# Two-partition block inversion, and transposes moved from TensorE to VectorE and DMA

## The chip, the cores and the metric

The kernel runs on one core of a Trainium2 chip. The metric is the device time of one execution in microseconds (us), taken as the median of several runs. A profile of one execution gives, for each engine, when each instruction ran and what it waited for. The engines are TensorE (PE in the profile; its weight loads are PEld), VectorE (DVE), ScalarE (ACT), GpSimd (POOL) and SyncE (SP, which here only issues transfers).

## The reference, cut to what matters

One step of a bidirectional hybrid layer: 384 tokens (128 context, 256 latent), width 2048, all in float32. An input projection feeds an RWKV-7 branch and a gated short convolution; both are projected, merged, projected again and added to the input. The scan is what the change touches, for 32 heads of size 64, in each of two directions:

```python
def step(S, inp):
    r_t, w_t, k_t, v_t, a_t, b_t = inp
    sa = jnp.einsum('dbhij,dbhj->dbhi', S, a_t)
    S = S * w_t[..., None, :] + sa[..., :, None] * b_t[..., None, :] + v_t[..., :, None] * k_t[..., None, :]
    y = jnp.einsum('dbhij,dbhj->dbhi', S, r_t)
    return S, y
```

The kernel computes it by chunks of 64 tokens. Inside a chunk the dependence of a token on the earlier ones is a strictly upper triangular 64x64 matrix, and the chunk needs the inverse of (identity minus that matrix).

## The kernel before, in words

**Two streams in one hand-written PE order.** A `Stream` object multiplies the activations with the weights (every product in three passes of float32r, `mm3`). One step of it is three matmuls of 128x128 by 384 columns; half a pair of weight columns is sixteen steps and one or two loads `raw` (1 MB together, `wload`, L96 to L106, two buffers), which ScalarE and VectorE split into a high and a low part (`whi`, `wlo`, L88 and L89, three buffers). The order of PE's instructions is the order of the program text; the other engines' order is made by a planner. The second stream is the scan, in sixteen blocks of two heads (128 channels). Its parts are generators: a `yield n` in them lets the weight stream do n steps (`drive`, L943). So the weight stream's steps stand between the scan's parts and hide their latencies.

**One block.** The main loop (L961) takes, in order:

- `prep_b` (L667): VectorE makes `pr` and `bk` (receptances and keys scaled by the decays), for two directions and six chunks each. PE multiplies them (`pA`, L703), VectorE masks the products into `A` (L709). The diagonal 32x32 blocks of A, 48 of them (two directions, two halves of a chunk, six chunks by two heads), are stored to a DRAM tile `ui` by SP (L713) and loaded back as `U` with one matrix on each of 48 partitions (L719). VectorE inverts there by thirty steps of two instructions, a product `ut` (L724) and an addition (L726). SP stores the inverses to `uo` (L729) and loads them into A (L734). VectorE then turns two of the four groups into `x11` (L737). GpSimd meanwhile multiplies `bk` by the chunk's last decay (L716).
- `prep_c` (L739): PE turns the values `v` (L763; reversed by a ScalarE copy, L760, for the second direction) and ten of the twelve key chunks of `bk` that the scan needs turned (L772); ScalarE copies both from PSUM into `sav` (L765) and `bt` (L773).
- `prep_a` of the next block (L608), after the stream has finished the pair `gv`; then the stream runs on until 80 steps (`WINDOW`) have gone by since `prep_b`.
- `scan` (L784): it begins with `pav` (L850), which reads the turned values, and `pH` (L842), the first matmul that reads `x11`; then come the chains over the chunks, which read `bt` (`pu`, L828). GpSimd clears part of A (L863).

`tc.issue_after(x)` makes what follows stand behind instruction x in the order of its engine.

Of the kernel before, what the change touches and what calls it, by code (L numbers as in the profile page):

```python
# [56 lines left out]
def hybrid_step(ctx, tc, cst, x_prompt, x_sample, state_f, state_b, c, c_ctx, ada_w, ada_b, norm_g,  # L57
# [38 lines left out]
    def wload(view, k0, cols, nm):  # L96

        w = P * len(cols)
        raw = wp.tile([P, 8, w], F32, tag="raw", name=f"raw_{nm}", bufs=2)
        if cols[-1] == cols[0] + P:  # L100
            nc.sync.dma_start(raw[:], view[:, k0:k0 + 8, cols[0]:cols[0] + 256])
        else:
            for i, c0 in enumerate(cols):
                nc.sync.dma_start(raw[:, :, i * P:(i + 1) * P], view[:, k0:k0 + 8, c0:c0 + P])
# [491 lines left out]
    def flat(a):  # L596
        return a.rearrange("p n t -> p (n t)")
# [4 lines left out]
    def hl_parts(t, hi, nm):  # L602
# [2 lines left out]
        V.tensor_tensor(lo[:], t[:], hi[:].bitcast(F32), ALU.subtract)  # L605
        return hi, lo

    def prep_a(b, o):  # L608

        bs = slice(b * P, (b + 1) * P)  # L610
        k = k_[b]
        kk = sp.tile([P, T], F32, tag="kk", name=f"kk_{b}")
        S.mul(kk[:], k[:], pcol(KK + b))
        sq = tmp(f"sq_{b}")
        S.activation(sq[:], kk[:], AF.Square)
        sqh, sql = hl_parts(sq, sp.tile([P, T], F32R, tag="hl", name=f"sqh_{b}"), f"sq_{b}")
# [50 lines left out]
    def prep_b(b, o):  # L667

        r, kk = r_[b], o["kk"]
        o["pr"], o["bk"] = [], []  # L670
        for d in range(2):
            ep, em, kd, bn = o["ep"][d], o["em"][d], o["kd"][d], o["bn"][d]
            pr = sp.tile([P, NCH, P], F32, tag=f"pr{d}", name=f"pr_{b}_{d}")
            bk = sp.tile([P, NCH, P], F32, tag=f"bk{d}", name=f"bk_{b}_{d}")
# [9 lines left out]
            o["bk"].append(bk)  # L684
        yield PB0

        def blocks(A, d, e):
# [9 lines left out]
        for d in range(2):  # L697
# [7 lines left out]
            for n0, w in ((0, 4), (4, 2)):  # L705
                mk = cs[:, m0:m0 + P].rearrange("p (w t) -> p w t", t=C).unsqueeze(1).broadcast_to([P, w, 2, C])
                for h in range(2):
                    f0 = NCH * d + n0
                    V.tensor_tensor(A[:, :, f0:f0 + w, hss[h]].rearrange("p w n t -> p n w t"),  # L709
                                    pas[h, n0][:, 0:w, :].rearrange("p n (w t) -> p n w t", t=C), mk, ALU.mult)  # L710
            yield PB1
            for e in range(2):
                nc.sync.dma_start(ui[d, e].rearrange("i s t -> s i t"), blocks(A, d, e))  # L713

        for d in range(2):
            G.tensor_tensor(o["bk"][d][:], o["bk"][d][:], o["ep"][d][:, :, C:C + 1].broadcast_to([P, NCH, P]), ALU.mult)  # L716

        U = sp.tile([48, 32, 32], F32, tag="U", name=f"U_{b}")
        nc.sync.dma_start(U[:], ui[:].rearrange("d e i s t -> (d e i) s t"))  # L719
        ut = sp.tile([48, 256], F32, tag="ut", name=f"ut_{b}")  # L720
        for s in range(1, 31):
            w = 31 - s
            tv = ut[:, 0:s * w].rearrange("p (a b) -> p a b", b=w)
            V.tensor_tensor(tv, U[:, 0:s, s:s + 1].broadcast_to([48, s, w]),  # L724
                            U[:, s:s + 1, s + 1:].broadcast_to([48, s, w]), ALU.mult)
            V.tensor_tensor(U[:, 0:s, s + 1:], U[:, 0:s, s + 1:], tv, ALU.add)  # L726
        dg = U[:].rearrange("p a b -> p (a b)")[:, 0:1024:33]
        V.tensor_scalar(dg, dg, 1.0, None, ALU.add)
        nc.sync.dma_start(uo[:].rearrange("d e i s t -> (d e i) s t"), U[:])  # L729
        x11 = sp.tile([64, 24, 32], F32, tag="x11", name=f"x11_{b}")  # L730
        o["x11"] = x11
        for e in range(2):
            for d in range(2):
                nc.sync.dma_start(blocks(A, d, e), uo[d, e].rearrange("i s t -> s i t"))  # L734

        for d in range(2):
            box["turned"] = V.transpose(x11[0:32, 12 * d:12 * d + 12, :], blocks(A, d, 0)).ins  # L737

    def prep_c(b, o):  # L739

        r, v, A = r_[b], v_[b], o["A"]

        s_in = sp.tile([P, 2, C], F32, tag="s_in", name=f"s_in_{b}")
        for d in range(2):
# [10 lines left out]
        for d in range(2):  # L755
            if d == 0:
                src = v
            else:
                src = tmp(f"vr_{b}")
                S.copy(src[:], v[:, ::-1])  # L760
            pv = bank(f"pv_{b}_{d}")
            for q in range(3):
                TE.transpose(pv[:, q, :], src[:, q * P:(q + 1) * P], ident)  # L763
# [3 lines left out]
        for d in range(2):  # L767

            for n0, n1 in (((0, 4), (4, 5)), ((0, 3), (4, 6)))[d]:
                pb = bank(f"pb_{b}_{d}_{n0}")  # L770
                for n in range(n0, n1):
                    TE.transpose(pb[:, n - n0, :], o["bk"][d][:, n, :], ident)  # L772
                S.copy(bt[:, NCH * d + n0:NCH * d + n1, :], pb[:, 0:n1 - n0, :])  # L773
                yield 1
# [397 lines left out]
```

## Time and profile before

| | us |
|---|---|
| median of 3 runs | 2236.57 (2234.74 to 2237.20) |
| the profiled execution | 2234.36 |
| its span, first to last instruction | 2232.6 |
| TensorE busy | 2173.1 (97%) |
| VectorE busy | 1553.3 (70%) |
| ScalarE busy | 1013.5 (45%) |
| GpSimd busy | 115.7 (5%) |

The mean granted TensorE clock is 0.998 of full speed. A row of a timeline has the start (us from the span's start), the duration in us, engine, line, operation, the tiles written and read, and in brackets the idle time before it with what ended that. A row of a group has the count after "x", then the busy time in us, the mean in ns, and the idle time before the group's instructions with its causes. Matmuls are pipelined, so that their listed durations overlap and only differences of starts tell what one costs.

### The profile page before, as it was taken

To read this page: it belongs to the slowest core of one execution; us is meant where nothing else is said; L and a number is where in the kernel's file an instruction comes from. 1 tells how busy PE (TensorE), PEld (TensorE's weight loads), DVE (VectorE), ACT (ScalarE), POOL (GpSimd) and SP (SyncE) were. 2 spreads that over 40 slices of the span, in tenths; PEclk is the share of its full clock that TensorE was granted. 3 is DMA by queue.
4 is the path that set the end of the run, shared out by engine and by line. 5 is a ranking of instruction groups with operands and counts; after the bars stand their busy time and mean duration, and the time that the engine had idled before them with its cause. 6 is when DMAs were issued, how large, how long until landed. Compare 5 with 4: busy or idle time off the path is not lost.

```text
span 2232.6 us, 40518 instructions
## 1 busy us (share of the span) xinstructions
PE 2173.1 (97%) x16020; PEld 2062.7 (92%) x16020; DVE 1553.3 (70%) x3240; ACT 1013.5 (45%) x1784; POOL 115.7 (5%) x113
## 2 busy tenths in 40 slices
PE   5999999999999999999999999999999999999998
PEld 3589999999999999999999999999999999998988
DVE  3259567787878878777878787887777785444354
ACT  4245435454545454444445454546454633333333
POOL 2000000000000000000000000000000000000000
PEclk9999999999999999999999999999999999999999
DMA  9974454444343435343444434344445464886633
GB/s 338 346 211 128 131 141 116 116 117 118 108 132 107 130 100 131 106 130 100 121 108 127 112 107 133 107 122 126 124 118 139 144 196 143 294 281 233 220 132 113
DMA packets 426574, 335.25 MB, mean 150 GB/s; under 512 B 82496, under 2 KB 408720, under 8 KB 425488
## 3 DMA queue, kind: packets, MB, share of 16 engines
q1 hardware_dynamic: 424896, 330.91, 50.2%
q8 instruction: 126, 2.06, 0.4%
q10 hardware_dynamic: 432, 1.57, 0.2%
q14 instruction: 64, 0.52, 0.1%
q0 software_dynamic: 1056, 0.19, 0.1%
HBM read 305.80 MB, written 26.21 MB: 149 GB/s over the span
## 4 chain that ended last, share of the span: by engine, by line
PE 74%; DVE 12%; DMA 6%; ACT 4%; issue 2%; SPq 1%; POOL 0%; POOLq 0%; DVEq 0%; ACTq 0%
DMA raw_adah<-in_ada_w_dram 4%; PE d_rk L81 3%; PE d_rk L82 3%; PE d_rk L83 3%; PE d_gv L81 3%; PE d_gv L82 3%; PE d_gv L83 3%; PE d_oa L81 2%; PE pA L703 2%; PE d_oa L83 2%; PE d_oa L82 2%; PE d_mb L81 2%; PE d_mb L83 2%; PE d_mb L82 2%; PE d_bc L81 2%
## 5 line engine op out<-in xcount | busy, mean ns | idle before, releaser
L724 DVE TENSOR_TENSOR ut<-U 48x30 f32<-48x30 f32 (+14 forms) x480 | 154.8, 323 | 18.3 <-DMA U<-ui 5.5
L81 PE MATMUL d_rk<-h_hi,whi_rk 128*128 128x384 f32 x480 | 161.7, 337 | 0.6 <-ACT lst L554 0.6
L726 DVE TENSOR_TENSOR U<-U,ut 48x30 f32<-48x30 f32 (+14 forms) x480 | 154.5, 322 | 11.1
L81 PE MATMUL d_gv<-h_hi,whi_gv 128*128 128x384 f32 x480 | 160.6, 335 | 0.0
L82 PE MATMUL d_rk<-h_lo,whi_rk 128*128 128x384 f32 x480 | 160.5, 334 | 0.0
L83 PE MATMUL d_rk<-h_hi,wlo_rk 128*128 128x384 f32 x480 | 160.4, 334 | 0.0
L83 PE MATMUL d_gv<-h_hi,wlo_gv 128*128 128x384 f32 x480 | 160.4, 334 | 0.0
L82 PE MATMUL d_gv<-h_lo,whi_gv 128*128 128x384 f32 x480 | 160.4, 334 | 0.0
L88 ACT CAST whi_gv<-raw_gv 128x1024 fp32r<-128x1024 f32 (+1 forms) x64 | 64.0, 999 | 139.6 <-PE d_rk L82 100.0
L88 ACT CAST whi_rk<-raw_rk 128x1024 fp32r<-128x1024 f32 x60 | 63.0, 1054 | 110.8 <-PE d_rk L82 34.7
L89 DVE TENSOR_TENSOR wlo_rk<-raw_rk,whi_rk 128x1024 fp32r<-128x1024 f32 x60 | 72.9, 1218 | 45.3 <-ACT whi_rk L88 35.6
L81 PE MATMUL d_bc<-h_hi,whi_bc 128*128 128x384 f32 x256 | 92.2, 360 | 0.0
L81 PE MATMUL d_gb<-h_hi,whi_gb 128*128 128x384 f32 x256 | 92.2, 360 | 0.0
L81 PE MATMUL d_bg<-h_hi,whi_bg 128*128 128x384 f32 x256 | 92.2, 360 | 0.0
L81 PE MATMUL d_bx<-h_hi,whi_bx 128*128 128x384 f32 x256 | 92.1, 360 | 0.0
L81 PE MATMUL d_ma<-h_hi,whi_ma 128*128 128x384 f32 x256 | 91.6, 358 | 0.0
L81 PEld LDWEIGHTS d_rk<-h_hi,whi_rk 128*128 128x128 f32 x480 | 90.1, 188 | 0.9 <-ACT lst L554 0.9
L81 PE MATMUL d_mb<-h_hi,whi_mb 128*128 128x384 f32 x256 | 90.4, 353 | 0.0
L81 PEld LDWEIGHTS d_gv<-h_hi,whi_gv 128*128 128x128 f32 x480 | 90.1, 188 | 0.2
L81 PE MATMUL d_ob<-ybh,whi_ob 128*128 128x384 f32 x256 | 88.4, 345 | 2.0 <-DVE smb L521 1.0
L82 PEld LDWEIGHTS d_rk<-h_lo,whi_rk 128*128 128x128 f32 x480 | 90.2, 188 | 0.0
L82 PEld LDWEIGHTS d_gv<-h_lo,whi_gv 128*128 128x128 f32 x480 | 90.1, 188 | 0.0
(315 smaller groups left out, 6548.4 us busy)
## 6 DMA issues: line engine op xcount, KB each, us to landing
raw_adah<-in_ada_w_dram SPq DMA_DIRECT2D x64, 512.0 KB, 8.7
raw_rk<-in_w_in_dram SPq DMA_DIRECT2D x60, 512.0 KB, 5.3
raw_gv<-in_w_in_dram SPq DMA_DIRECT2D x60, 512.0 KB, 4.9
raw_ma<-in_w_in_dram SPq DMA_DIRECT2D x16, 1024.0 KB, 5.6
raw_mb<-in_w_in_dram SPq DMA_DIRECT2D x16, 1024.0 KB, 5.6
raw_bc<-in_w_in_dram SPq DMA_DIRECT2D x16, 1024.0 KB, 5.5
raw_bx<-in_w_in_dram SPq DMA_DIRECT2D x16, 1024.0 KB, 5.4
raw_bg<-in_w_in_dram SPq DMA_DIRECT2D x16, 1024.0 KB, 5.5
```

What stands on the lines that cost most here:

```text
L81: TE.matmul(out, wh, xh, start=start, stop=False)
L82: TE.matmul(out, wh, xl, start=False, stop=False)
L83: TE.matmul(out, wl, xh, start=False, stop=stop)
L88: S.copy(hi[0:rows], src)
L89: V.tensor_tensor(lo[0:rows], src, hi[0:rows].bitcast(F32), ALU.subtract)
L703: TE.matmul(pas[h, n // 4 * 4][:, n % 4, :], bk[hss[h], n, :], pr[hss[h], n, :], start=True, stop=True)
L724: V.tensor_tensor(tv, U[:, 0:s, s:s + 1].broadcast_to([48, s, w]), U[:, s:s + 1, s + 1:].broadcast_to([48, s, w]), ALU.mult)
L726: V.tensor_tensor(U[:, 0:s, s + 1:], U[:, 0:s, s + 1:], tv, ALU.add)
```

## The change

- The 48 matrices are inverted on 96 partitions. `un` holds all rows of every matrix twice, on partitions 0 to 47 and 64 to 111; `ux` holds the even rows on the first group and the odd rows on the second. A step updates up to half as many rows in each partition. Four loads take the place of one, and the added diagonal takes two instructions.
- The inverses are stored by two transfers and loaded back by four, all issued by GpSimd instead of SP. `x11` lies in `un`.
- PE's sixteen transposes a block and the ScalarE copies behind them go. VectorE's 32x32 transposes turn the blocks of the values (into `vt`) and of all twelve key chunks (in place, in `bks`); SP then places the blocks with transfers from SBUF to SBUF: eight for the values (behind the loads of `ux`) and sixteen for the keys (four at a time, behind the latest weight load), each of 32 partitions by twelve runs of 128 bytes.
- `prep_c` lets the weight stream go on 24 and 16 steps before the first and the second half of the key transfers, where it had seven single steps in all.

```diff
@@ wload @@
+                x = nc.sync.dma_start(raw[:, :, i * P:(i + 1) * P], view[:, k0:k0 + 8, c0:c0 + P])
+        box["raw"] = x.ins
@@ before prep_a @@
+    un = sp.tile([112, 32, 32], F32, tag="un", name="un")
+    ux = sp.tile([112, 16, 32], F32, tag="ux", name="ux")
+    G.memset(un[:], 0.0)
+    G.memset(ux[:], 0.0)
@@ prep_b @@
+        bks = sp.tile([P, 2, NCH, P], F32, tag="bk", name=f"bk_{b}")
+        o["bk"] = [bks[:, d] for d in range(2)]
...
+        vt = sp.tile([P, 2, T], F32, tag="vt", name=f"vt_{b}")
+        with tc.issue_after(last):
+            for d in range(2):
+                V.transpose(vt[:, d], v_[b][:, ::-1] if d else v_[b][:])
+            for d in range(2):
+                V.transpose(flat(bks[:, d]), flat(bks[:, d]))
-        U = sp.tile([48, 32, 32], F32, tag="U", name=f"U_{b}")
-        nc.sync.dma_start(U[:], ui[:].rearrange("d e i s t -> (d e i) s t"))
+        for g in range(2):
+            nc.sync.dma_start(un[64 * g:64 * g + 48], ui[:].rearrange("d e i s t -> (d e i) s t"))
+        for g in range(2):
+            o["loaded"] = nc.sync.dma_start(ux[64 * g:64 * g + 48], ui[:].rearrange(
+                "d e i (m g) t -> (d e i) m g t", g=2)[:, :, g, :]).ins
         for s in range(1, 31):
-            w = 31 - s
-            tv = ut[:, 0:s * w].rearrange("p (a b) -> p a b", b=w)
-            V.tensor_tensor(tv, U[:, 0:s, s:s + 1].broadcast_to([48, s, w]),
-                            U[:, s:s + 1, s + 1:].broadcast_to([48, s, w]), ALU.mult)
-            V.tensor_tensor(U[:, 0:s, s + 1:], U[:, 0:s, s + 1:], tv, ALU.add)
+            w, m = 31 - s, (s + 1) // 2
+            tv = ut[:, 0:m * w].rearrange("p (a b) -> p a b", b=w)
+            V.tensor_tensor(tv, ux[:, 0:m, s:s + 1].broadcast_to([112, m, w]),
+                            un[:, s:s + 1, s + 1:].broadcast_to([112, m, w]), ALU.mult)
+            V.tensor_tensor(ux[:, 0:m, s + 1:], ux[:, 0:m, s + 1:], tv, ALU.add)
-        nc.sync.dma_start(uo[:].rearrange("d e i s t -> (d e i) s t"), U[:])
+        for g in range(2):
+            dg = ux[64 * g:64 * g + 48].rearrange("p a b -> p (a b)")[:, g:512:34]
+            V.tensor_scalar(dg, dg, 1.0, None, ALU.add)
+            G.dma_start(uo[:].rearrange("d e i (m g) t -> (d e i) m g t", g=2)[:, :, g, :],
+                              ux[64 * g:64 * g + 48])
+        x11 = un[0:64, 0:24, :]
         for e in range(2):
             for d in range(2):
-                nc.sync.dma_start(blocks(A, d, e), uo[d, e].rearrange("i s t -> s i t"))
+                G.dma_start(blocks(A, d, e), uo[d, e].rearrange("i s t -> s i t"))
@@ prep_c @@
-            for q in range(3):
-                TE.transpose(pv[:, q, :], src[:, q * P:(q + 1) * P], ident)
-                S.copy(sav[C:P, NCH * d + e:NCH * d + NCH:2, :], pv[C * e:C * e + C, 0:3, :])
-                for n in range(n0, n1):
-                    TE.transpose(pb[:, n - n0, :], o["bk"][d][:, n, :], ident)
-                S.copy(bt[:, NCH * d + n0:NCH * d + n1, :], pb[:, 0:n1 - n0, :])
-                yield 1
+        x = o["vt"][:].rearrange("p d (n e t) -> p (d n) e t", e=2, t=32)
+        with tc.issue_after(o["loaded"]):
+            for e in range(2):
+                for q in range(4):
+                    nc.sync.dma_start(sav[C + 32 * e:C + 32 * e + 32, :, 32 * q:32 * q + 32],
+                                      x[32 * q:32 * q + 32, :, e, :])
+        x = o["bks"][:].rearrange("p d n t -> p (d n) t")
+        for p in range(4):
+            if p % 2 == 0:
+                yield (24, 16)[p // 2]
+            with tc.issue_after(box["raw"]):
+                for q in range(4):
+                    nc.sync.dma_start(bt[32 * p:32 * p + 32, :, 32 * q:32 * q + 32],
+                                      x[32 * q:32 * q + 32, :, 32 * p:32 * p + 32])
```

More of the change, by code (lines that the diff above doesn't have):

```diff
@@ L100, in wload @@
         if cols[-1] == cols[0] + P:
-            nc.sync.dma_start(raw[:], view[:, k0:k0 + 8, cols[0]:cols[0] + 256])
+            x = nc.sync.dma_start(raw[:], view[:, k0:k0 + 8, cols[0]:cols[0] + 256])
         else:
             for i, c0 in enumerate(cols):
-                nc.sync.dma_start(raw[:, :, i * P:(i + 1) * P], view[:, k0:k0 + 8, c0:c0 + P])
+                x = nc.sync.dma_start(raw[:, :, i * P:(i + 1) * P], view[:, k0:k0 + 8, c0:c0 + P])
+        box["raw"] = x.ins
         res = [split(raw[:, 4 * q:4 * q + 4, :], [P, 4, w], "whi", "wlo", wp, f"{nm}_{q}") for q in range(2)]
@@ L669, in prep_b @@
         r, kk = r_[b], o["kk"]
-        o["pr"], o["bk"] = [], []
+        o["pr"] = []
+        bks = sp.tile([P, 2, NCH, P], F32, tag="bk", name=f"bk_{b}")
+        o["bk"] = [bks[:, d] for d in range(2)]
         for d in range(2):
@@ L673, in prep_b @@
             pr = sp.tile([P, NCH, P], F32, tag=f"pr{d}", name=f"pr_{b}_{d}")
-            bk = sp.tile([P, NCH, P], F32, tag=f"bk{d}", name=f"bk_{b}_{d}")
+            bk = o["bk"][d]
             V.tensor_tensor(bk[:, :, 0:C], c3(bn[:]), c3(em[:]), ALU.mult)
@@ L683, in prep_b @@
             o["pr"].append(pr)
-            o["bk"].append(bk)
         yield PB0
@@ L708, in prep_b @@
                     f0 = NCH * d + n0
-                    V.tensor_tensor(A[:, :, f0:f0 + w, hss[h]].rearrange("p w n t -> p n w t"),
-                                    pas[h, n0][:, 0:w, :].rearrange("p n (w t) -> p n w t", t=C), mk, ALU.mult)
+                    last = V.tensor_tensor(A[:, :, f0:f0 + w, hss[h]].rearrange("p w n t -> p n w t"),
+                                           pas[h, n0][:, 0:w, :].rearrange("p n (w t) -> p n w t", t=C), mk,
+                                           ALU.mult).ins
             yield PB1
@@ L715, in prep_b @@
         for d in range(2):
-            G.tensor_tensor(o["bk"][d][:], o["bk"][d][:], o["ep"][d][:, :, C:C + 1].broadcast_to([P, NCH, P]), ALU.mult)
-        U = sp.tile([48, 32, 32], F32, tag="U", name=f"U_{b}")
-        nc.sync.dma_start(U[:], ui[:].rearrange("d e i s t -> (d e i) s t"))
-        ut = sp.tile([48, 256], F32, tag="ut", name=f"ut_{b}")
-        for s in range(1, 31):
-            w = 31 - s
-            tv = ut[:, 0:s * w].rearrange("p (a b) -> p a b", b=w)
-            V.tensor_tensor(tv, U[:, 0:s, s:s + 1].broadcast_to([48, s, w]),
-                            U[:, s:s + 1, s + 1:].broadcast_to([48, s, w]), ALU.mult)
-            V.tensor_tensor(U[:, 0:s, s + 1:], U[:, 0:s, s + 1:], tv, ALU.add)
@@ L727, in prep_b @@
-        dg = U[:].rearrange("p a b -> p (a b)")[:, 0:1024:33]
-        V.tensor_scalar(dg, dg, 1.0, None, ALU.add)
-        nc.sync.dma_start(uo[:].rearrange("d e i s t -> (d e i) s t"), U[:])
-        x11 = sp.tile([64, 24, 32], F32, tag="x11", name=f"x11_{b}")
+            G.tensor_tensor(bks[:, d], bks[:, d], o["ep"][d][:, :, C:C + 1].broadcast_to([P, NCH, P]), ALU.mult)
+        vt = sp.tile([P, 2, T], F32, tag="vt", name=f"vt_{b}")
[4 more added lines that the diff above has]
+                V.transpose(flat(bks[:, d]), flat(bks[:, d]))
@@ new lines, in prep_b @@
+        o["bks"], o["vt"] = bks, vt
+        for g in range(2):
[3 more added lines that the diff above has]
+                "d e i (m g) t -> (d e i) m g t", g=2)[:, :, g, :]).ins
+        ut = sp.tile([112, 128], F32, tag="ut", name=f"ut_{b}")
+        for s in range(1, 31):
+            w, m = 31 - s, (s + 1) // 2
[3 more added lines that the diff above has]
+            V.tensor_tensor(ux[:, 0:m, s + 1:], ux[:, 0:m, s + 1:], tv, ALU.add)
@@ L739, in prep_c @@
     def prep_c(b, o):
-        r, v, A = r_[b], v_[b], o["A"]
+        r = r_[b]
         s_in = sp.tile([P, 2, C], F32, tag="s_in", name=f"s_in_{b}")
@@ L754, in prep_c @@
         o["sav"], o["bkt"] = sav, bt
[L755 to L761, printed above, removed]
-            for q in range(3):
-                TE.transpose(pv[:, q, :], src[:, q * P:(q + 1) * P], ident)
-            for e in range(2):
-                S.copy(sav[C:P, NCH * d + e:NCH * d + NCH:2, :], pv[C * e:C * e + C, 0:3, :])
-            yield 1
-        for d in range(2):
-            for n0, n1 in (((0, 4), (4, 5)), ((0, 3), (4, 6)))[d]:
-                pb = bank(f"pb_{b}_{d}_{n0}")
-                for n in range(n0, n1):
-                    TE.transpose(pb[:, n - n0, :], o["bk"][d][:, n, :], ident)
-                S.copy(bt[:, NCH * d + n0:NCH * d + n1, :], pb[:, 0:n1 - n0, :])
-                yield 1
+        x = o["vt"][:].rearrange("p d (n e t) -> p (d n) e t", e=2, t=32)
+        with tc.issue_after(o["loaded"]):
+            for e in range(2):
+                for q in range(4):
[9 more added lines that the diff above has]
+                                      x[32 * q:32 * q + 32, :, 32 * p:32 * p + 32])
         ks = o["kd"]
```

## The prediction

> **What bounds the kernel now.** I read the page first, then the groups of TensorE by line and form, then the timeline of one block of the main loop.
>
> ```profile
> PE 2173.1 (97%) x16020; PEld 2062.7 (92%) x16020; DVE 1553.3 (70%) x3240; ACT 1013.5 (45%) x1784; POOL 115.7 (5%) x113
> ...
> q1 hardware_dynamic: 424896, 330.91, 50.2%
> ```
>
> TensorE is busy in 97% of the span; the next engine has 70%. The groups of TensorE say whether its own waits are worth anything (last column: idle time before the group, all instances).
>
> ```profile
> L772 PE MATMUL pb<-cs,bk 128*128 128x128 f32 x160 | 27.9, 272 | 0.2 <-issue 0.2
> ...
> L842 PE MATMUL pH<-x,A 32*32 32x32 f32 x768 | 10.1, 194 | 0.0
> ...
> L763 PE MATMUL pv<-cs,vr 128*128 128x128 f32 x48 | 7.9, 272 | 1.4 <-DVE A L709 1.4
> L763 PE MATMUL pv<-cs,v 128*128 128x128 f32 x48 | 7.8, 271 | 0.0
> ```
>
> pH is the first matmul that reads the inverse. Over sixteen blocks it waited 0.0 us, so the inversion hides fully today, and what the PE is given to do is what the loop lasts. The PE's order is written out by hand: it cannot do other work when pH is not ready. So a saving on PE counts in full, and so does lateness of the inverse beyond its slack.
>
> **What goes from PE.** Sixteen transposes a block (six on L763, ten on L772). Their listed 272 ns overlap with their neighbours; the net price is a difference of starts:
>
> ```profile
> 423.97 0.34 PE L83 MATMUL d_bx<-h_hi,wlo_bx 128*128 128x384 f32 x1
> ...
> 425.86 0.60 PE L772 MATMUL pb<-cs,bk 128*128 128x128 f32 x4
> ...
> 426.82 0.27 PE L772 MATMUL pb<-cs,bk 128*128 128x128 f32 x1
> ...
> 428.72 0.33 PE L82 MATMUL d_rk<-h_lo,whi_rk 128*128 128x384 f32 x1
> ...
> 430.13 0.33 PE L81 MATMUL d_rk<-h_hi,whi_rk 128*128 128x384 f32 x1
> ...
> 439.49 0.33 PE L81 MATMUL d_rk<-h_hi,whi_rk 128*128 128x384 f32 x1
> ```
>
> A weight matmul takes (439.49 - 430.13) / 54 = 0.1733 us when nothing interrupts. From 423.97 to 428.72 lie all sixteen transposes and seventeen such steps: 4.75 - 17 x 0.1733 = 1.80 us, 0.11 each, as the group of four against the single one has it ((0.60 - 0.27) / 3 = 0.11). Sixteen blocks give 28.8 us. Nine ScalarE copies a block (turned tiles and reversed v) go too; ScalarE, at 45%, bounds nothing, so I price them at nothing.
>
> The steps between part B and the scan stay the same: part C yields 41 instead of 7, but the loop then goes on until the gv pair is done and up to 80 steps, so only the place of part A within the stretch can move. But pH is reached 1.8 us sooner, and that is the catch: the inverse has to come sooner too.
>
> **The path of the inverse, one block.**
>
> ```profile
> 525.58 1.95 DVE L709 TENSOR_TENSOR A<-pA,cs 128x512 f32<-128x512 f32 x4 [0.65 <-PE pA L703]
> ...
> 530.59 0.44 SPq L719 DMA_DIRECT2D U<-ui  x1
> ...
> 534.47 1.23 DVE L89 TENSOR_TENSOR wlo_rk<-raw_rk,whi_rk 128x1024 fp32r<-128x1024 f32 x1 [4.48 <-ACT whi_rk L88]
> 535.62 0.18 DVE L724 TENSOR_TENSOR ut<-U 48x30 f32<-48x30 f32 x1
> ...
> 549.38 0.40 DVE L724 TENSOR_TENSOR ut<-U 48x240 f32<-48x240 f32 x1
> ...
> 564.66 0.21 DVE L726 TENSOR_TENSOR U<-U,ut 48x30 f32<-48x30 f32 x1
> ...
> 567.93 1.88 SPq L734 DMA_DIRECT2D A<-uo  x4
> ...
> 574.00 1.02 DVE L737 STREAM_TRANSPOSE x<-A 32x384 f32<-32x384 f32 x2 [2.69 <-DMA A<-uo]
> ...
> 577.31 0.62 PE L842 MATMUL pH<-x,A 32*32 32x32 f32 x48
> ```
>
> The first of the two turns ends near 574.5, pH starts at 577.31: slack 2.8 us. I read the same pair of rows in the fourteen blocks from the third on; the tightest and the loosest:
>
> ```profile
> 681.65 1.02 DVE L737 STREAM_TRANSPOSE x<-A 32x384 f32<-32x384 f32 x2 [2.15 <-DMA A<-uo]
> 682.37 0.76 PE L842 MATMUL pH<-x,A 32*32 32x32 f32 x48
> ...
> 1726.86 1.03 DVE L737 STREAM_TRANSPOSE x<-A 32x384 f32<-32x384 f32 x2 [1.20 <-DMA A<-uo]
> 1731.65 0.62 PE L842 MATMUL pH<-x,A 32*32 32x32 f32 x48
> ```
>
> Slack runs from 0.2 to 4.3 us (the first two blocks have far more). Taken as evenly spread, an inverse that is x us later against pH costs the fourteen blocks 14 (x - 0.2)^2 / 8.2 us up to x = 4.3, and 14 (x - 2.25) above. Now x, part by part.
>
> *Inversion.* 210 more elements take 0.40 - 0.18 = 0.22 us: 1.05 ns each. Sixty instructions handle 2 sum s(31 - s) = 9,920 elements now and 2 sum ceil(s/2)(31 - s) = 5,200 after, since even and odd rows lie on two partition groups: 4,720 x 1.05 = 5.0 us sooner. The diagonal takes a second 0.2 us instruction.
>
> *Turning on VectorE.* Two of 128x384 at 0.51 us (the 32x384 rows at 574.00) and two of 128x768, at twice that: 3.1 us. The row at 534.47 shows 4.48 us idle right where they fall, after L709, so I take nothing; bounds 0 and 3.1, if the planner puts them ahead of a wlo that PE needs. The keys also wait for GpSimd's multiplication, which follows the same matmuls.
>
> *Loads.* One U becomes two un (as large as U) and two ux of 768 runs of 128 B. SP issues three more at 0.44 us before the last, and the extra U-sized copy takes its turn on the engines: I take 1.7 us later; bounds 0 (in this block U landed behind a wlo anyway) and 3.
>
> *Store and reload on GpSimd's queue.* Landing medians, and GpSimd's issue times:
>
> ```profile
> ui<-A SPq DMA_DIRECT2D x64, 48.0 KB, 2.1
> U<-ui SPq DMA_DIRECT2D x16, 192.0 KB, 5.1
> ...
> uo<-U SPq DMA_DIRECT2D x16, 192.0 KB, 4.7
> A<-uo SPq DMA_DIRECT2D x64, 48.0 KB, 3.6
> ...
> out_dram<-ns SPq DMA_DIRECT2D x128, 8.0 KB, 1.5
> ...
> m5g<-in_ada_b_dram POOLq DMA_DIRECT2D x4, 2.0 KB, 4.9
> ...
> DMA to landing us min/median/max: 2.7/5.5/6.1
> ...
> 1.96 0.53 POOL L237 DMA_DIRECT2D prow<-in_mu_next_dram  x1
> 2.47 0.50 POOL L238 DMA_DIRECT2D prow<-in_norm_g_dram  x1
> ```
>
> Today's tail is 4.7 + 3.6 = 8.3 us. GpSimd's small transfers land 2.7 to 6.1 us after issue (that line is of L284), where SP's small ones take 1.5. Issue is 0.53 us for 48 rows and 0.50 for 16, about 1 ns a run: 1.25 us for 768, 0.87 for 384. The turn needs both stores and the first two loads. For the landing I take 4.2, nearer m5g's 4.9 than the idle 2.7, because a 1 MB weight load is mostly in flight then. Tail: 1.25 + 4.2 + 0.7 + 0.87 + 4.2 + 0.4 = 11.6 us, 3.3 later than now (0.7 and 0.4 for the longer descriptions). Bounds with 2.7 and 6.1: 0.3 and 7.1 later.
>
> The Trainium skill ("DMA: Bandwidth & Descriptors", Latency and other measured facts) gives about 1 us to the first byte for GpSimd's transfers against 0.6 for SP's: by it the two hops would be only 0.8 us longer, x would fall to about -0.5 and the time to 2208. The trace shows a wider difference, 4.9 against 1.5, so I stay with that.
>
> *Sum.* x = 3.3 + 1.7 + 0.2 + 1.8 - 5.0 = 2.0. Stall: 14 x 1.8^2 / 8.2 = 5.5 us. Net 28.8 - 5.5 = 23.3 us. The profiled execution has 2234.4 us around a span of 2232.6, 0.1% under the median of 2236.6; it becomes 2211, and the median **2213 us** (-1.0%).
>
> *SP's other new transfers.* Sixteen for the keys, eight for the values, 384 runs of 128 B each. At U's 0.44 us that is 10.6 us of issue a block in batches of eight: 3.5 us in front of a weight load. On the engines, the average packet costs 16 x 2232.6 x 0.502 / 424896 = 42 ns, so 9,216 runs take at most 24 us of a block's 105, against 50% use. A load of 16 steps (8.3 us) lands in about 5.5 and feeds a further two-slot ring of split weights, so I count nothing; cover gone, 3.5 us a batch, two or three a block. SP loses the wait for the inversion's end (uo, A<-uo), behind which weight loads stood. On GpSimd only the memset of A and the next block's key multiplication stand behind the new waits, both later than pH.
>
> **The rivals.**
>
> *A: the PE work goes, small stalls (0 to 12 us).* Time 2207 to 2220.
>
> *B: the inverse is later, x between 2.8 and 4.2.* Stall 12 to 27 us, time 2220 to 2236. For it: the GpSimd median of 5.5 would give a tail of 14.2 and x = 4.6, its far end. Against: that was the prologue with the engines full.
>
> *C: slower. GpSimd's descriptions of 768 and 384 short runs take longer than the row count says.* No row has more than 48. Equality is at x = 4.3, when each of the four DMAs ahead of the turn takes 0.6 us more than I took. If each is held for one wlo (1.2 us), x = 6.8: stall 64 us, time 2272. What speaks against it:
>
> ```profile
> 1958.58 0.49 POOL L284 DMA_DIRECT2D m5g<-in_ada_b_dram  x1 [59.26 <-DVE m5l L89]
> ...
> 1958.74 0.55 DVE L1057 TENSOR_TENSOR sma<-sma,d_oa 128x384 f32<-128x384 f32 x1
> ```
>
> The issue kept its 0.49 us beside VectorE. The Trainium skill ("SBUF — State Buffer", SBUF: two separate sides) says that GpSimd cannot write descriptors while VectorE runs an instruction in a 2-port mode, until it ends. That is this rival's mechanism; the row agrees with it only so far as two-input instructions are let through, and the work beside the inversion is mostly of that kind.
>
> *D: weight loads come late behind SP's batches.* Two batches a block, 3.5 us each uncovered: 2208 + 16 x 7 = 2320. Against: 8.3 us between loads and the ring behind them.
>
> *E: no gain, since VectorE's chain through the scan sets the pace and PE only fills.* 2232 to 2241. Against: PE's idle before pH and pb is 0.0 and 0.2.
>
> **How the numbers follow.** A 0.56, B 0.19, C 0.13, D 0.05, E 0.07. A alone spans 2207 to 2220; with B it holds 0.75, and E's lower half brings it to 8 in 10: 2204 to 2238, three us under A's floor for waits on ScalarE that may go as well. A measurement here tells 0.2% (4.5 us) from no change. Faster: A and nearly all of B, 0.75; same: E and the edge of B, 0.08; slower: C and D, 0.17.
>
> **What would show it.** L763 and L772 gone from PE's groups and its busy time down by some 29 us; the sixty inversion instructions at a mean near 240 ns instead of 323; the four transposes lying in VectorE's idle time ahead of them; GpSimd's issues near 1.25 and 0.87 us; a new wait of PE, pH on the turn, near 5 us in total and none elsewhere. I am wrong if pH's wait is over 29 us, if GpSimd's tail is over 14 us or under 8.5, or if matmuls of weights wait on wlo.

## The result, and the profile after

The changed kernel takes 2426.5 us (2425.9 to 2429.1) against 2236.5: a ratio of 1.085, interval 1.0837 to 1.0864, or 190 us more. The forecast was 2213, in 2204 to 2238. The profiled span, 2426.8 us, is that of the slowest of the four executions.

The page's busy line of the changed kernel, and the spans with the mean granted clock of the changed kernel and of the kernel before:

```profile
PE 2233.7 (92%) x15764; PEld 2105.4 (87%) x15764; DVE 1539.6 (63%) x3320; ACT 951.1 (39%) x1640; POOL 180.5 (7%) x211
```
```profile
core 0: 2426.8 us, clock 0.957
```
```profile
core 0: 2232.6 us, clock 0.998
```

256 matmuls are gone, as planned, yet PE is busy 61 us longer: the clock accounts for up to (1 - 0.957) x 2426.8 = 104 us at full speed, against 4 us before. And PE stands idle 2426.8 - 2233.7 = 193 us, against 59.5. So there are some 134 us of new waits and up to 100 us of lost clock, less the 28.8 us of the transposes. That is 205 where 194 were measured: the terms overlap by about 10 us. TensorE's waits (engine, tile, line, whom it waited for; total, times, longest):

```profile
PE d_gv L81 <- ACT whi_gv L88: 48.9, 14, 6.0
...
PE d_gv L83 <- DVE wlo_gv L89: 19.2, 14, 2.1
PE d_bg L81 <- ACT whi_bg L88: 8.9, 3, 3.0
```

pH, the only wait I had forecast, is not among them. What is late is split weights: those of gv, and of the pair behind gv, in fourteen of the sixteen blocks. (rk, gv, gb, bg and the like are pairs of weight columns, `zs` is ScalarE's copy of finished sums out of PSUM.) One such block by stretches of 2 us (length of the stretch; busy time and count of PE, PEld, VectorE, ScalarE and GpSimd; the granted clock; the DMA engines' load and GB/s):

```profile
817.00:819.00 2.00, 2.00 (x14) 2.00 (x13) 1.86 (x8) 0.96 (x2) 0.00 (x0) 1.00 0.52 74
819.00:821.00 2.00, 0.44 (x3) 0.12 (x1) 2.00 (x9) 1.52 (x4) 0.00 (x0) 1.00 0.84 221
...
823.00:825.00 2.00, 0.47 (x1) 0.47 (x2) 2.00 (x5) 0.88 (x2) 0.00 (x0) 0.50 1.48 141
825.00:827.00 2.00, 2.00 (x8) 2.00 (x8) 1.86 (x6) 0.42 (x1) 0.00 (x0) 0.50 0.50 59
```

PE stops at 819.4. Apart from three matmuls it stands until 825, and then 8 matmuls touch a stretch instead of 14: the clock is at 0.50. Now who was late. The queue of SP in the same block (start, time of all issues together, count):

```profile
801.35 0.39 SPq L104 DMA_DIRECT2D raw_gv<-in_w_in_dram  x1
...
804.22 7.42 SPq L782 DMA_DIRECT2D sav<-vt  x8
811.69 0.61 SPq L104 DMA_DIRECT2D raw_gv<-in_w_in_dram  x1
812.39 5.24 SPq L791 DMA_DIRECT2D bt<-bk  x8
817.73 1.18 SPq L104 DMA_DIRECT2D raw_gv<-in_w_in_dram  x2
818.96 6.01 SPq L791 DMA_DIRECT2D bt<-bk  x8
825.82 8.10 SPq L101 DMA_DIRECT2D raw_gb<-in_w_in_dram  x2
```

The moves take 18.7 us of SP a block, in batches of 5.2 to 7.4 us, and the two column halves of one gv load are issued 10.3 us apart. But read on to ScalarE, which casts what lands:

```profile
817.39 0.48 ACT L418 COPY zs<-d_rk 128x384 f32<-128x384 f32 x1 [9.52 <-PE d_rk L83]
...
820.73 2.00 ACT L88 CAST whi_gv<-raw_gv 128x1024 fp32r<-128x1024 f32 x2
...
843.05 0.48 ACT L418 COPY zs<-d_gv 128x384 f32<-128x384 f32 x1 [1.59 <-PE d_gv L83]
...
844.87 2.94 ACT L88 CAST whi_gb<-raw_gb 128x1024 fp32r<-128x1024 f32 x3
```

The first raw_gb was issued at 825.82, and loads of that tile in this stretch land 5.6 to 5.8 us after issue: it was there by 831.6. It was cast at 844.87, behind a copy of the finished gv sums, which cannot start before PE ends gv at 843. PE therefore ran out of weights at 843.0 although they had lain in SBUF for 11 us. (One of the three buffers that it needs was free by about 834.4, an estimate: gv's fourth cast, at 830.39, had waited until its first was used up, and the second lasts 24 more matmuls of 0.173 us.) The casts and the copies stand in an order fixed when the kernel is built. Before the change the casts came first; after it, in fourteen of fifteen blocks, they come behind the copies of the rk sums. ScalarE before:

```profile
546.10 1.06 ACT L88 CAST whi_gv<-raw_gv 128x1024 fp32r<-128x1024 f32 x1 [3.11 <-PE d_rk L82]
548.35 0.48 ACT L417 COPY zs<-d_rk 128x384 f32<-128x384 f32 x1 [1.20 <-PE d_rk L83]
...
566.89 1.05 ACT L88 CAST whi_bx<-raw_bx 128x1024 fp32r<-128x1024 f32 x1 [1.41 <-PE d_gv L82]
567.85 0.47 ACT L417 COPY zs<-d_gv 128x384 f32<-128x384 f32 x1
```

So there are two suspects, SP's time and that order, and the experiments have to part them.

The parts of the inverse's way that I priced (VectorE's groups; line, shapes, count, busy us and mean ns; then GpSimd's issues in the block):

```profile
L744 DVE TENSOR_TENSOR ut<-ux,un 112x30 f32<-112x30 f32 (+7 forms) x480 | 119.4, 249 | 18.4 <-DMA ux<-ui 4.9 <-DMA sav<-vt 0.3
...
L731 DVE STREAM_TRANSPOSE bk<-bk 128x768 f32<-128x768 f32 x32 | 30.2, 950 | 0.0
L729 DVE STREAM_TRANSPOSE vt<-v 128x384 f32<-128x384 f32 x32 | 16.6, 554 | 0.0
```
```profile
831.47 1.50 POOL L750 DMA_DIRECT2D uo<-ux  x2 [32.93 <-DVE ux L746]
836.08 2.45 POOL L756 DMA_DIRECT2D A<-uo  x4 [3.11 <-DMA uo<-ux]
```

### The profile page after: what moved, and what is told of

Its sections match the earlier page's. It is cut to its first block, busy times and chain, and to the rows that moved or that the text cites. A ratio compares the mean times of both kernels' runs of the same rounds, so it can differ in the third digit from the quotient of the medians.

```text
span 2426.8 us, 40572 instructions
## 1 busy us (share of the span) xinstructions
PE 2233.7 (92%) x15764; PEld 2105.4 (87%) x15764; DVE 1539.6 (63%) x3320; ACT 951.1 (39%) x1640; POOL 180.5 (7%) x211
## 3 DMA queue, kind: packets, MB, share of 16 engines
q1 hardware_dynamic: 577984, 349.80, 52.7%
q0 software_dynamic: 4640, 6.48, 1.5%
## 5 line engine op out<-in xcount | busy, mean ns | idle before, releaser
L81 PE MATMUL d_gv<-h_hi,whi_gv 128*128 128x384 f32 x480 | 175.3, 365 | 48.9 <-ACT whi_gv L88 48.9
L83 PE MATMUL d_gv<-h_hi,wlo_gv 128*128 128x384 f32 x480 | 175.4, 365 | 19.2 <-DVE wlo_gv L89 19.2
L82 PE MATMUL d_gv<-h_lo,whi_gv 128*128 128x384 f32 x480 | 172.8, 360 | 0.0
L81 PEld LDWEIGHTS d_gv<-h_hi,whi_gv 128*128 128x128 f32 x480 | 100.6, 210 | 53.6 <-ACT whi_gv L88 53.4
L744 DVE TENSOR_TENSOR ut<-ux,un 112x30 f32<-112x30 f32 (+7 forms) x480 | 119.4, 249 | 18.4 <-DMA ux<-ui 4.9
L746 DVE TENSOR_TENSOR ux<-ux,ut 112x30 f32<-112x30 f32 (+7 forms) x480 | 119.3, 249 | 14.2 <-DVE ut L744 0.2
L83 PEld LDWEIGHTS d_gv<-h_hi,wlo_gv 128*128 128x128 f32 x480 | 99.6, 207 | 25.2 <-DVE wlo_gv L89 25.2
L82 PEld LDWEIGHTS d_gv<-h_lo,whi_gv 128*128 128x128 f32 x480 | 99.9, 208 | 0.0
L83 PE MATMUL d_ma<-h_hi,wlo_ma 128*128 128x384 f32 x256 | 89.1, 348 | 6.0 <-DVE wlo_ma L89 6.0
L83 PE MATMUL d_ob<-ybh,wlo_ob 128*128 128x384 f32 x256 | 88.1, 344 | 7.1 <-DVE wlo_ob L89 7.1
```

The costliest lines, as they stand in the source:

```text
L81: TE.matmul(out, wh, xh, start=start, stop=False)
L82: TE.matmul(out, wh, xl, start=False, stop=False)
L83: TE.matmul(out, wl, xh, start=False, stop=stop)
L744: V.tensor_tensor(tv, ux[:, 0:m, s:s + 1].broadcast_to([112, m, w]), un[:, s:s + 1, s + 1:].broadcast_to([112, m, w]), ALU.mult)
L746: V.tensor_tensor(ux[:, 0:m, s + 1:], ux[:, 0:m, s + 1:], tv, ALU.add)
```

## The experiments

Theories: (1) SP's issues in front of weight loads; (2) full DMA engines; (3) the order of ScalarE and VectorE, planned around the new transfers; (4) a PE gap beyond about 2 us costs more than itself, since the clock halves behind it. (The expectations of e3 and e4 call something else the third theory: that the loss lies in the inversion.) Each time below is a median of four runs, ten for e9, beside the kernel before at 2236.5 to 2237.7 on the same chip. Line numbers in the profile lines are those of the kernel that ran; the diffs are cut to what matters and partly written shorter than the code.

| run | time, us | ratio (interval) |
|---|---|---|
| turning alone, SP (e3) | 2455.5 | 1.0972 (1.0954 to 1.0991) |
| inversion alone (e4) | 2292.6 | 1.0253 (1.0237 to 1.0268) |
| the same, turn of the inverse later (e9) | 2236.8 | 0.9998 (0.9988 to 1.0007) |
| moves by GpSimd (e1) | 2338.3 | 1.0451 (1.0435 to 1.0468) |
| moves on SP, spread (e6) | 2336.6 | 1.0445 (1.0430 to 1.0461) |
| batches, rk casts first (e2) | 2427.3 | 1.0850 (1.0832 to 1.0869) |
| spread, rk casts first (e7) | 2320.5 | 1.0375 (1.0360 to 1.0391) |
| batches, order half mended (e12) | 2441.2 | 1.0900 (1.0878 to 1.0922) |
| spread, order mended (e13) | 2260.2 | 1.0095 (1.0079 to 1.0112) |
| batches, order mended throughout (e14) | 2265.6 | 1.0128 (1.0113 to 1.0143) |
| spread, order mended throughout (e15) | 2247.2 | 1.0045 (1.0028 to 1.0062) |
| added gap of 1.2 us a block (s1) | 2265.6 | 1.0131 (1.0113 to 1.0148) |
| added gap of 3.5 us a block (s2) | 2325.7 | 1.0395 (1.0378 to 1.0412) |
| moves by GpSimd, inverse by SP (e8) | 2271.4 | 1.0157 (1.0142 to 1.0172) |
| the same, keys turned later (e11) | 2313.8 | 1.0348 (1.0331 to 1.0366) |
| turning with GpSimd's moves, old inversion (e10) | **2220.1** | 0.9923 (0.9908 to 0.9937) |

### One half at a time

e3 keeps the old inversion with SP's store and loads and does the turning with its 24 moves; e4 keeps PE's transposes and takes the new inversion with GpSimd's queue.

```diff
# e3                                     # e4
-un, ux, two partition groups, G store   -vt, bks turned; sav, bt by 24 moves
+U[48, 32, 32], SP store and loads       +pv, pb by TE.transpose and S.copy
```

> The kernel before with the turning part of the change alone: no PE transposes, VectorE's turns and SP's 24 transfers; the inversion on 48 partitions with its one load, SP's store and reload stay. Theories 1 and 2: the loss comes with this part, 2400 to 2440 (VectorE's longer inversion may add to it). A third theory, that the loss lies in the inversion part (four loads, GpSimd's store and reload): 2205 to 2225.

> The kernel before with the inversion part alone: even and odd rows on two partition groups, four loads, store and reload by GpSimd; PE's transposes and the copies behind them stay. Theories 1 and 2: no batch on SP, PE's work as before, so 2236 within 6 us. The third theory (loss in the inversion part): over 2300. My prediction's term for GpSimd's tail (3.3 us later) with 5.0 us off the inversion would leave pH at its slack: 2236 within 6 us too.

The turning alone is as bad as the whole change and 29 us worse (15 us above what I expected), so the damage lies there. But my expectation for e4 failed by 56 us. PE waits 34.8 us, in 15 blocks, at pl, the matmul of `prep_a` that reads the small split weight lwl. VectorE in one of them:

```profile
909.43 0.57 DVE L747 STREAM_TRANSPOSE un<-A 32x384 f32<-32x384 f32 x1 [3.52 <-DMA A<-uo]
909.93 0.50 DVE L605 TENSOR_TENSOR lo_sq<-sq,sqh 128x384 fp32r<-128x384 f32 x1
910.37 0.40 DVE L89 TENSOR_TENSOR lwl<-lraw,lwh 96x256 fp32r<-96x256 f32 x1
```

VectorE stands 3.52 us at the turn of the inverse until A lands, with lwl behind it; lwl's input was cast by 905.9. Before the change lwl stood ahead of the turn. e9 restores that and nothing else:

```diff
-            box["turned"] = V.transpose(x11[...], blocks(A, d, 0)).ins      # in prep_b
+        with tc.issue_after(box["lo"]): box.pop("turn")()                   # in prep_a, behind lwl
```

> The kernel before plus the new inversion with GpSimd's queue (2292.6 in its own run, 34.8 us of PE waiting at pl for lwl), with one more edit: the turn of the inverse is put behind prep_a's second split on VectorE. Theory 'order': VectorE, in order, stood at the turn until the inverse's load landed (909.4 in the block I read) with lwl behind it; with the order mended the pl waits and the halved clock go, and the time is that of the kernel before, 2232 to 2245. Rival: the GpSimd queue makes the inverse late whatever the order, and the wait moves to pH: 2265 to 2295.

2236.8: the whole loss of e4 was one instruction's place. With PE's transposes in place, the inversion, its loads and GpSimd's queue cost nothing when the order is right.

### Which queue

```diff
# e1                                         # e6 (SP): three moves, then eight steps, and so on
-nc.sync.dma_start(sav[...]) and bt[...]     -batches of eight
+nc.gpsimd.dma_start(...)                    +for i in range(0, 24, 3): yield 8; three moves
```

> The changed kernel with its 24 transfers within SBUF a block issued by GpSimd instead of SP; the same runs of 128 bytes cross the same 16 engines. Theory 1 (SP's issue time: batches of eight at 0.62 us or more stand in front of a weight load on SP, the split weights come late, PE waits): the waits of d_gv on whi_gv vanish, about 118 us of PE's idle time and 99 us of halved clock go, and the time is 2236.5 - 28.5 plus a few us for pH: 2208 to 2218. Theory 2 (the 9,216 short runs fill the engines): the weight loads stay late whichever queue issues them, 2380 to 2430.

> The changed kernel with SP's 24 transfers in eight groups of three, one group for every eight steps of the weight stream, each behind the weight load that was issued last. Theory 1: at 0.62 us each a group puts 1.9 us in front of a load that has more than that to spare, so the waits on whi go: 2208 to 2225. Theory 2: the same runs on the engines, 2380 to 2430. Theory 1 with the planner's order of ScalarE as a cause of its own (casts put behind the copies of d_rk): some of the waits stay, 2250 to 2350.

Both come down by some 90 us. e1 lies between its two theories; e6 lies where I had put theory 1 with the planner's order as a cause of its own. In e1 the waits at gv are gone; what remains is the inverse, now late (PE's largest wait in e1; the profile names no releaser, but pH starts 0.1 us behind the turn of the inverse):

```profile
PE pH L860 <- issue: 51.4, 14, 8.8
```

But e1 proves neither theory, since it changes three things at once. SP's time is free. The planner orders ScalarE's casts as before: ahead of the copies, in all fifteen blocks. And the packets are not the same: SP's queue shows 577,984 in the changed kernel and 153,600 fewer in e1, while GpSimd's goes from 4,640 to only 12,288 more, for the same bytes. The DMA queues of e1, SP's and GpSimd's (packets, MB, share of the engines):

```profile
q1 hardware_dynamic: 424384, 330.91, 50.9%
q0 software_dynamic: 16928, 25.38, 6.2%
```

e6 has the same 24 issues on SP as the changed kernel and the same packets, so theory 2 falls with it: 2336.6, where full engines would have kept it at 2380 or more.

### Issue or order

e2 is the changed kernel with the copies of the rk sums put behind the first gv cast; e7 is e6 with that edit.

```diff
         def consume(i, ps):
-            take_shifted("rk"[i], ...)
+            with tc.issue_after(box["cast0"]):
+                take_shifted("rk"[i], ...)
```

> The changed kernel, all of its transfers in place; ScalarE's order alone is changed: the copies of the finished rk sums (zs, which wait for the last d_rk matmul) come behind the casts of the first half of the gv weights, as they did before the change. Theory 'order': the planner, which took the weight loads for late, put zs ahead of the casts, and ScalarE stands there for up to 9.5 us with the cast behind it; then most of the 68 us of d_gv waits and the clock spells behind them go: 2330 to 2375. Theory 'issue alone': the weights land only at 816.5 in the block I read, against zs at 817.4, so the order costs 1 us or so a block: 2400 to 2430.

> The moves stay on SP in groups of three every eight steps (as in the spread run, 2336.6), and ScalarE's order is mended as in the run beside it. In the spread run the gv weights were issued at 997.7 to 998.9 and their cast ran at 1010.0, behind zs, which waited until 1009.2. Theory 'order': the 38 us of d_gv waits on wlo and about half as much of halved clock go: 2275 to 2300. Theory 'issue alone': the spread run's remaining waits are SP's time, and nothing moves: 2325 to 2340.

e2 gives the number of the issue theory, for another reason: the wait moved. ScalarE has cast the first half of gv by 820.4, and VectorE splits it 5 us later (e2):

```profile
825.25 0.24 DVE L750 TENSOR_TENSOR ut<-ux,un 112x84 f32<-112x84 f32 x1
825.42 1.23 DVE L91 TENSOR_TENSOR wlo_gv<-raw_gv,whi_gv 128x1024 fp32r<-128x1024 f32 x1
```

All instructions of VectorE from the landing (818.3) up to the split are the inversion's, one after the other: wlo_gv stands behind them in the order. e7 fell between its two theories, with the second half of gv split behind the end of the inversion. So e12 (batches) puts the inversion's columns from 14 on behind the first gv half's split, and e13 (spread) does so for both halves and puts kk behind the casts:

```diff
-        for s in range(1, 31): ...                       # all in prep_b
+        o["steps"](1, 14)                                # in prep_c
+            with tc.issue_after(box["wl"]): o["steps"](14, 31); o["close"]()   # 24 steps on
```

> The changed kernel with its moves in batches of eight on SP, ScalarE's casts first (as in the earlier run, 2427), and now VectorE's order mended as well: the second half of the inversion (from column 14) is put behind the split of the first half of the gv weights. There VectorE had that split 5 us behind the cast (820.4 against 825.4), behind 22 steps of the inversion. Theory 'order': SP's issue time alone nearly hides, as I had predicted, and what costs is the planner's order of ScalarE and VectorE together; the 72 us of d_gv waits fall below 25 and the halved clock with them: 2270 to 2340. Theory 'issue': the weights land late in fact, and the wait stays at the cast or moves to the next pair: 2390 to 2430.

> The spread moves (groups of three on SP) with ScalarE's casts first (2320.5), and both halves of the gv weights' splits put ahead of the second half and the last steps of the inversion; kk comes behind the casts on ScalarE. In the run before, the second half's weights were issued at 1001.3, cast at 1015.6 behind kk and split at 1019.8 behind the end of the inversion, while TensorE waited. Theory 'order': the 42 us of d_gv waits and the halved clock (48 us) go, and only the inverse's slack is left: 2225 to 2275. Theory 'issue': 2305 to 2325.

e13 falls by 60 us, as the order theory had it. e12 rises by 14 us, above both of its theories. Its profile says why: the wait moved again, to the second half of gv, which VectorE splits only when the inversion is all but over, 4.6 us after both its casts had ended, and the pair behind gv is still cast behind the gv sums (ScalarE, then VectorE, in e12):

```profile
831.73 1.04 ACT L90 CAST whi_gv<-raw_gv 128x1024 fp32r<-128x1024 f32 x1
...
849.72 0.48 ACT L424 COPY zs<-d_gv 128x384 f32<-128x384 f32 x1 [1.59 <-PE d_gv L83]
...
851.54 2.94 ACT L90 CAST whi_gb<-raw_gb 128x1024 fp32r<-128x1024 f32 x3
```
```profile
836.94 0.19 DVE L755 TENSOR_TENSOR ux<-ux,ut 112x30 f32<-112x30 f32 x1
...
837.38 1.23 DVE L91 TENSOR_TENSOR wlo_gv<-raw_gv,whi_gv 128x1024 fp32r<-128x1024 f32 x1
```

e14 and e15 mend every place that had been seen to hold finished data: casts of gv and of the pair behind it ahead of the copies of sums, kk (the scaled keys of `prep_a`) behind the casts, both splits ahead of the rest of the inversion, the turn behind lwl. Moves and queues are those of the change (e14) or spread (e15).

```diff
+            with tc.issue_after(box["cast0"]): take_gate(...) or take_shifted("v", ...)
+            piece(14, 25) behind gv's first half, piece(25, 31) behind its second
+            with tc.issue_after(box["lo"]): turn()
```

> The changed kernel's work and queues unchanged (24 moves a block in batches of eight on SP, the inverse on GpSimd's queue); the order of ScalarE and VectorE mended at every place that held a finished load in the runs so far: the casts of the gv weights and of the pair behind them come ahead of the copies that wait for the sums before them, kk behind the casts, the splits of both gv halves ahead of the rest of the inversion, the turn of the inverse behind prep_a's split. In the run with half of this (2441) the second half's weights were issued at 824.0 and had 4.8 us to land, but were cast at 830.8 and split at 837.4, and the next pair's load of 831.0 was cast at 851.5. Theory 'order': SP's issue time by itself is nearly hidden and the time falls below 2300, most likely 2235 to 2290. Theory 'issue': late landings keep the gaps, 2370 or more.

> The same mended order with the moves in groups of three on SP (2260.2 before the last two edits). Theory 'order': the remaining waits at gv (11 us) and pl (5 to 9) shrink and PE's saving shows: 2215 to 2245. Theory 'issue': SP's 15 to 19 us a block still make weights late here and there, 2250 to 2265.

e14 is the changed kernel's work, transfer for transfer (577,984 packets on SP's queue, as there), and takes 2265.6: 161 of the 190 us were order. SP's batches are as long as ever, but less waits for them (SP in a block of e14, then PE's wait at gv):

```profile
755.81 7.78 SPq L804 DMA_DIRECT2D sav<-vt  x8
763.64 0.61 SPq L106 DMA_DIRECT2D raw_gv<-in_w_in_dram  x1
764.34 5.24 SPq L822 DMA_DIRECT2D bt<-bk  x8
```
```profile
PE d_gv L83 <- DVE wlo_gv L91: 24.7, 17, 2.4
```

Batches against spread moves are worth 18 us (2265.6 - 2247.2). e15 falls between its two theories. It is still 11 us slower than the kernel before and 34 above the forecast: PE idles 84 us against 59.5 (the largest new wait is 8.7 at gv), and the mean clock is 0.993. No run takes these last waits apart.

### What a gap costs

In the kernel before, a PE transpose right behind pH waits for GpSimd's memset of A and nothing (s1) or four more memsets (s2).

```diff
         G.memset(A[C:P, 0, :, :], 0.0)
+        (s2: four memsets of jk[128, 512])
+        G.memset(jk[:, 0:64], 0.0)
+        TE.transpose(pj[0:64, 0, :], jk[:, 0:64], ident)
```

> The kernel before, with one added wait a block and nothing else: behind pH, TensorE turns a tile that GpSimd has just cleared, right behind its clearing of A (1.38 us, begun when the pav matmuls end). TensorE then stands some 1.2 to 1.5 us in each of the sixteen blocks. Theory 'clock': a gap under about 1.6 us leaves the granted clock at 1.0, so the price is the gap itself: 19 to 24 us, 2255 to 2262. Rival: every gap costs as much as it lasts and nothing more, whatever its length; the same number here, so the run beside it decides. If even this gap halves the clock: 2270 or more.

> As the run beside it, with four more clearings of a 128x512 tile ahead of the turn (0.46 us each by 0.9 ns an element), so the gap is 3 to 3.5 us a block, 48 to 56 us in all. Theory 'clock': each such gap is followed by one or two spells of 3.41 us at half the granted clock, which cost 1.7 or 3.4 us more: 2312 to 2348. Rival 'a gap costs what it lasts': 2285 to 2295.

The waits added, s1 and s2, and the stretches with and behind one gap of s2:

```profile
PE pj L871 <- POOL jk L869: 19.4, 16, 1.2
```
```profile
PE pj L871 <- POOL jk L869: 56.7, 16, 3.5
```
```profile
926.00:930.00 4.00, 0.46 (x17) 0.35 (x7) 0.71 (x2) 2.51 (x6) 3.34 (x6) 0.93 0.54 183
930.00:932.00 2.00, 2.00 (x8) 2.00 (x8) 0.00 (x0) 0.00 (x0) 0.00 (x0) 0.50 0.00 0
```

16 gaps of 3.54 us cost 88.6 us, 5.5 each; 16 of 1.21 us cost 28.5 (ratio interval 1.0113 to 1.0148), 1.8 each. In the trace's records of the clock all sixteen gaps of s2 are followed by 0.50, ten for 6.83 us and six for 3.41, which is 44 us lost; gaps and clock make 101, so 12 came back elsewhere. In s1 six of the sixteen are followed by 3.41 us, which I had put at none: 19.4 + 6 x 1.7 = 29.6. Theory 4 stands, without the threshold: some gaps of 1.2 us are enough.

### Toward a better version

e8 changes the two queues over: moves by GpSimd, inverse by SP, the turn behind lwl. e11 is e8 with the keys turned behind the inversion. e10 has e8's moves and turn with the inversion, store and loads of before.

```diff
# e8                               # e11                                  # e10
-G: uo, A<-uo; SP: sav, bt         -V.transpose(bks) ahead of inversion   -un, ux, four loads
+SP: uo, A<-uo; G: sav, bt         +behind its last instruction           +U, one load
```

> The two queues changed over: the 24 moves a block on GpSimd's queue, the inverse stored and loaded back by SP; the turn of the inverse (which waits for that load) is put behind prep_a's second split of lw on VectorE. If the costs are where I now put them (SP's issue time in front of weights; the GpSimd tail of 10 to 13 us beside its moves, 51 us of pH waits; VectorE held by the turn with lwl behind it, 15 us of pl waits), all three go, PE's 28.8 us stay saved, and 10 to 25 us of small waits remain: 2210 to 2240, at or below the kernel before. Rival: the inversion itself ends too late since the turning and the moves share VectorE and the engines with it: pH still waits 2 us or more a block, 2270 to 2310.

> The run with the queues changed over (2271.4), with the turning of the keys (two of 128x768 on VectorE) put behind the inversion's last instruction, where VectorE waits for the inverse's way through memory, and their sixteen moves behind it. Theory 'the front is too full': the inversion starts sooner (12.5 us behind the masks instead of 14.2) and lasts nearer 24 us than 27.8, so the sigmoid products (20 us of waits), pl (9) and pH (8) come in time: 2220 to 2250. Rival: the keys' moves (16 x 0.62 us and 3 to 4 us to land) come too late for the first pu matmul some 8 us behind pH, which then waits 2 to 5 us a block: 2275 to 2330.

> The turning alone: the inversion, its store and its loads as before the change (48 partitions, SP), the keys and values turned by VectorE, and the 24 moves a block issued by GpSimd's idle queue; the turn of the inverse is put behind prep_a's split on VectorE. PE saves its 28.8 us. Theory: with neither SP nor the order in the way only the inverse's slack is at stake: 1.8 us of median slack before, 1.8 us less since PE comes sooner, and the longer inversion against one load instead of four: pH waits 0 to 2 us a block, 2212 to 2240. Rival: the turning on VectorE and 9,216 short packets beside U's load put the inversion back as in the other GpSimd runs (first instruction 14 us behind the masks instead of 8): pH waits 3 us or more a block with halved clock behind them, 2265 to 2310.

e8 missed by 31 us, within its rival's range: pl, pH and the sigmoid products still make PE wait, 1 to 3 us at a time. e11's time is in its rival's range, but not by the rival's way: PE waits 0.3 us at pu for the keys, and 60.2 us at pH, since the turn of the inverse starts 15.3 us behind the inversion's end (8.3 in e8, medians); what holds it up there stays open. e10 is 0.8% faster than the kernel before. Its page line, its waits and GpSimd's issues:

```profile
PE 2151.2 (97%) x15764; PEld 2039.4 (92%) x15764; DVE 1590.2 (72%) x3304; ACT 954.4 (43%) x1640; POOL 350.6 (16%) x497
```
```profile
PE pl L83 <- DVE lwl L91: 4.2, 7, 1.7
PE pH L857 <- DVE x L755: 2.2, 1, 2.2
```
```profile
L788 POOL DMA_DIRECT2D bt<-bk x256 | 156.1, 616 | 77.4 <-DMA sav<-vt 41.5 <-DMA bt<-bk 30.2 <-issue 5.2
```

PE's busy time is down by 21.9 us, 28.8 less what the mean clock of 0.995 gave back, and idle is up by 5. As in e1, the queue, the order and the packets differ at once from e3's, so e10 shows that the turning pays in this arrangement, not which of the three makes it pay.

## Why the prediction was wrong, point by point

The step that failed is the cover of SP's other new transfers, "so I count nothing". The bullets take the terms one by one. First the inverse's way, from the masks' end to pH: medians over thirteen blocks from the third on, from the starts and ends of the same rows in each trace ("turn's end" is that of the second turn; the prediction's slack was read from the first).

| us | before | e9 | after | e10 |
|---|---|---|---|---|
| masks to first inversion instruction | 8.2 | 12.5 | 11.3 | 9.0 |
| inversion, first to last | 29.3 | 23.9 | 21.7 | 31.1 |
| end to turn | 8.1 | 10.1 | 9.0 | 6.1 |
| turn's end to pH | 1.8 | 2.0 | 18.4 | 1.0 |

- *What goes from PE:* right. Taken alone and out of others' way (e10) it brings 17 us.
- *Inversion, 5.0 us sooner:* 5.4 (29.3 - 23.9). The instructions have a mean of 249 ns; I had near 240.
- *Loads, 1.7 us, bound 3:* about right. The first step of the inversion starts 4.3 us later in e9, but only 1.5 of that is the loads: the diagonal's addition, which waits for the last `ux` in ten of the thirteen blocks, starts 9.7 us behind the masks, where the first step before the change started at 8.2. The other 2.8 us are a split of rk weights that stands between in VectorE's order, which the prediction had no term for. One block of e9:

```profile
539.23 0.17 DVE L742 TENSOR_SCALAR ux<-ux 48x16 f32<-48x16 f32 x1 [1.38 <-DMA ux<-ui]
541.00 1.23 DVE L91 TENSOR_TENSOR wlo_rk<-raw_rk,whi_rk 128x1024 fp32r<-128x1024 f32 x1 [1.60 <-ACT whi_rk L90]
542.15 0.18 DVE L737 TENSOR_TENSOR ut<-ux,un 112x30 f32<-112x30 f32 x1
```

- *Store and reload on GpSimd's queue, 3.3 us later:* 2.0 in e9. Issues were 0.75 and 0.61 us, not 1.25 and 0.87, and the transfers landed in medians of 3.8 and 2.2 us there, not 4.2 each. The Trainium skill's figure ("DMA: Bandwidth & Descriptors", Latency and other measured facts) gave 0.8 by my estimate; the measurement lies between.
- *x without PE's 1.8:* 0.2 forecast, 0.9 measured in e9 (4.3 + 2.0 - 5.4): that it is so near is in part luck, since the tail was put too high and VectorE's 2.8 us at nothing. With the order mended e9 stands at the time of before, as the prediction's formula has it (14 x 0.7^2 / 8.2 = 0.8 us). In the changed kernel x never mattered: PE itself came later, and 18.4 us of slack opened in front of pH.
- *Turning, 3.1 us on VectorE:* (30.2 + 16.6) / 16 = 2.9.
- *Rival C:* GpSimd issued 384 runs in 0.61 us, as fast as SP's median of 0.62. The hold-up that the Trainium skill ("SBUF — State Buffer", SBUF: two separate sides) describes for 2-port work of VectorE does not show in the mean of 616 ns over 256 issues in e10, with VectorE at 72%. Which of VectorE's instructions here are of that kind, no run shows.
- *SP's other new transfers, "so I count nothing":* this is the step that failed, and with it "a new wait of PE, pH on the turn, ... and none elsewhere". The price was low: 18.7 us in the block shown instead of 10.6, in three batches. The cover was counted on SP and the DMA engines alone, and even so it was not nothing: with the order mended the batches cost 18 us (e14 against e15), and e14 stands 53 us above the forecast. What I left out is larger, 161 us: the engines which take up the loads run in a fixed order, planned with the transfers in the queue, and with the moves on SP it put copies, inversion and turn ahead of casts and splits. The prediction had named the sign itself (matmuls of weights that wait on wlo). I named the planner for the 3.1 us of turning only. In the trace of before the warning was there to read: ScalarE's cast of the next weights stood just ahead of the copies of the finished sums.
- *Rival D* (0.05, 2320) had the right place, weights late behind SP's batches. It priced the gap, 7 us a block, and not the clock behind it, and gave SP's time as the cause where most of the loss was order.
- *A gap's price:* my terms for stalls (14 (x - 0.2)^2 / 8.2 and D's 16 x 7) took 1 us lost for 1 us waited. s2 has 5.5 us for 3.5.

How the 161 us of order split among the six places mended in e14 is open; they were not undone one by one.

## What to carry to other kernels

Where a planner fixes the order of the engines, price a new transfer twice: what it takes on its queue, and what the planner will now put ahead of the instruction that takes up a load. Look in the trace for finished data: issue plus landing against the start of its consumer; if the consumer starts much later and its engine was idle or held by something else, the order is to be mended and not the transfer. Try an idle queue for a large batch of small moves (e10), and count a TensorE gap of 1 to 4 us at one and a half times its length (1.8 us for 1.2 and 5.5 for 3.5 here).

## What was not expected of the hardware

- After a gap the granted clock is 0.50 for spells of 3.41 us or a multiple (in the changed kernel 22 of 33 are of 6.83, three of 10.24). The Trainium skill ("TensorE: Matmul & The Clock Gate", Part 1: The HAM clock gate) describes a free-running window of 3413 ns and half rate, which agrees. It has the drop after at least one idle window; here 6 of 16 gaps of 1.21 us were followed by one.
- A move of 384 runs of 128 B within SBUF takes about 0.62 us to issue on SP and on GpSimd alike, against 0.44 for U's load before. On SP's queue the profile shows each run as a packet of its own, on GpSimd's packets of 3072 bytes: 153,600 against 12,288 for the same moves, with the 4-byte packets that go along.
